# A hybrid layer's state-space part: a second unit's input in lent tiles, a shorter step table, and one GELU in place

## The chip, the cores and the metric

The kernel runs on one core of one Trainium2 chip. Its engines work side by side, each through its own list of instructions: PE (TensorE) multiplies matrices, DVE (VectorE), ACT (ScalarE) and POOL (GpSimd) do elementwise work, and SP (SyncE) issues transfers (DMAs). POOL and ACT may issue transfers too. An engine that waits holds back all that is queued behind on its own list. What counts is the time of one execution on the device, in microseconds (us). Weight loads of PE are listed as PEld.

## The reference

One layer with 2048 frames, 1024 channels and float32 values. Two groups of heads share one normalisation and one input projection; their outputs share an output projection.

```python
h = rmsnorm(x, norm_mix_g[l])
proj = h @ w_in[l]                       # 512 columns u, then q, k, v of 512 each
y_ssm = s5_mixer(u_ssm, ...)
y_att = chunked_attention(q, k, v, attn_rel_bias[l])
mixed = concatenate([rmsnorm(y_ssm, ...), rmsnorm(y_att, ...)])
x = x + mixed @ w_out[l]
h2 = rmsnorm(x, norm_ffn_g[l])
x = x + (silu(h2 @ w_gate[l]) * (h2 @ w_up[l])) @ w_down[l]
return rmsnorm(x, norm_final_g)
```

The state-space mixer is a complex diagonal recurrence over the frames, then `y = gelu(C x + D u)` and `y * sigmoid(y @ w_glu + b_glu)`. The attention looks at the own chunk of 64 frames and the eight before it, with 8 heads of 64.

## The kernel before

**Stages.** After a prologue (input projection `u`, tables of the recurrence) come the attention with the state-space layer woven into it, then the mix phase (GELU, GLU, output projection), then the feed-forward part.

**Steps.** `att_phase` runs 128 steps: 4 blocks of 512 frames, 4 pairs of heads, 2 heads, 4 tiles of queries. A step issues the scores of its tile (PE `sc`, then DVE L866, which adds the bias and takes the minimum for the exponent, then the exponential on ACT, L869) and the transposes of the step two earlier: PE writes them to the bank `pt`, ACT casts a high part `pth` (L884), DVE subtracts a low part `ptl` (L885). Matrices are multiplied in three products of high and low parts. Products with the values (`pj`) and the scaling of a pair of heads (`rb`, DVE L918, stored to `ya_s` by SP, L919) follow when a head or a pair is through.

**Units.** Everything else that belongs under the attention is cut into `Unit`s: generators with a first and a last step. At each step every unit is advanced in proportion. Projections of the next block (`hT`, `qk`, `v` units), eight pairs of state-space units (`ssm_front`, `ssm_back`) and the start of the mix phase are such units. The tables SX and SY give the first steps of the eight fronts and backs.

A front loads the input `U` (128x1024) and the weights `Bst`, multiplies them (PE `pj<-U,Bst`), copies the result into `X` (ACT L584), and POOL runs the recurrence in place on `X` (L598 to L601 steps of a scan, L609 and L610 carries). At its end POOL issues four transfers of the states into `XG` (L632). The back loads `Tm` and `Vm`, multiplies `U` by `Tm` and `XG` by `Vm` into `pj`, ACT copies the sum over `U` (L652), and SP stores that as `y` (L654). Even units from 2 on keep `U` in the space of `rsn`; all others share one buffer `U`, so that unit 1's load must follow unit 0's store.

**Order.** PE's instructions keep the order of the program. Those of DVE, ACT, POOL and SP are ordered by the Tile framework's scheduler, except where the code pins one. Tiles come from pools; the pool `aw` holds the tiles of the projections, `ssm` those of the state-space units. A pool that is released gives its space to the next.

**Mix phase.** It opens at step 119 (OPEN), where `aw` is released, and advances from step 122 (GSTART) as a unit of 26 parts. `fetch` reads `y` for two blocks of 64 chunks into `yr` (L1038), `load` turns it into `ys` by a GELU that reads with a stride (L1050), then splits `ys` into `gh` and `gl`. `glu` multiplies by `w_glu` (split into `wgh` and `wgl`), applies the sigmoid (L1079) to the whole block and multiplies. Newton steps (L98 to L111) make the inverse root of the mean square for a block, `spread` lays it across partitions by transposes of `no`, `rstd2` multiplies with it, `mixed` splits the result for `w_out`. Block 0's `w_out` starts with two held first halves: PE does the four rows of weights that belong to the attention's output, and the second half when the state-space part is there. ACT applies one function table at a time: changing between the exponential and the GELU shows as ACT_TABLE_LOAD.

Of the kernel before, what the change touches and what calls it, by code (L numbers as in the profile page):

```python
# [34 lines left out]
WB = 3  # L35
OPEN, GSTART = 119, 122
R1 = 13
SGB = 2
RA1, RA2 = 2, 12
QS = 4, 5, 6, 7, 0, 1, 2, 3  # L40
# [519 lines left out]

def ssm_front(k, p, psum, S, b, eng):

# [15 lines left out]
    for q in range(GP):  # L578
        ps = k.t(psum, "pj", [P, 2, NC], bufs=2)
        for g2 in range(2):  # L580
            k.ta.matmul(ps[:, g2, :], bst[:, 2 * q + g2, :], U[:, 2 * q + g2, :], start=True, stop=True)
        for g2 in range(2):
            for c in range(2):
                nc.scalar.copy(X[g2 * NS : (g2 + 1) * NS, c, q, :], ps[c * NS : (c + 1) * NS, g2, :])  # L584
        yield
# [74 lines left out]
ST = 2, 10  # L660
SX = 4, 24, 35, 48, 61, 74, 87, 100
SY = 20, 36, 49, 62, 75, 88, 101, 114

# [23 lines left out]
def att_phase(k, ident, S, aw, x0, roots):  # L687

    tc, nc, io, pfs = k.tc, k.nc, k.io, k.pfs
    with ExitStack() as cx:  # L690
# [265 lines left out]
        for b in range(NG // GB):  # L956
            units.append(Unit(ssm_front(k, sp, psum, S, b, k.ssm_eng), SSM_F, SX[b], SX[b] + 9, SX[b] - 2 if b == 0 else 2 if b == 1 else 5, light=SL))
# [23 lines left out]

PY, PZ = 8, 1
MIX_N = 17 + PY + PZ


def mix_phase(k, S, bank):
# [3 lines left out]
    with ExitStack() as cx:  # L990
# [48 lines left out]

        def load(sb, one=False):  # L1040
            b = B()
            b.o = {}
            yt = k.t(my, "ys", [P, 4, SB], bufs=2)
            b.ys, b.g = [yt[:, f] for f in range(4)], []
            if sb and sb % 2 == 0:
                fetch(sb)
            yv = b.yr = yrs[0][:, :, :, (sb % 2) * 64 : (sb % 2 + 1) * 64]
            fs = [slice(0, 4)] if one else [slice(f, f + 1) for f in range(4)]
            for s in fs:
                nc.scalar.activation(yt[:, s].rearrange("p f (c j) -> p f c j", j=L), yv[:, s].rearrange("p f j c -> p f c j"), AF.Gelu_apprx_tanh)  # L1050
            for f in range(4):
# [48 lines left out]
        def big():  # L1100
            return k.t(psum, *BIG)
# [42 lines left out]
        def next_block(sb):  # L1144
            b = load(sb)
            load_a(b, sb)
# [18 lines left out]
        b = load(0, True)  # L1165
        load_a(b, 0)
        raws = [load_wo(n, wr, "xt") for n in range(2)]
        for _ in range(PY):
            yield
        for n, _ in enumerate(glu(b, bank, True)):  # L1170
            if n == RA1:
# [5 lines left out]
            yield  # L1177
        nxt = load(1, True)
        for _ in range(PZ):
            yield  # L1180

# [16 lines left out]
        for sb in range(NSB):  # L1198
# [3 lines left out]
            if sb == 0:  # L1202
                held = [w_out(0, b, 2 * n) for n in range(2)]
                next(held[0])
                ps = big()
                spread(k, te, ps[:, :512], b.o[1], 0)
                with tc.high_priority():
                    rstd2(b, 1, ps[:, :512])
                    mixed(b, 1)
                next(held[1])  # L1210
            else:
                mixed(b, 1)
            for n in range(4):
                if n == 0 and 0 < sb < NSB - 1:
                    nxt = next_block(sb + 1)
                if sb or n > 1:
                    for _ in w_out(sb, b, 2 * n):
# [519 lines left out]
```

## Time and profile before

| | us |
|---|---|
| median of three runs | 2264.51 |
| lowest and highest run | 2261.2, 2265.51 |
| the profiled execution, time | 2267.91 |
| the profiled execution, span | 2266.1 |
| PE busy | 2165.6 (96% of the span) |
| DVE busy | 1542.4 (68%) |
| ACT busy | 1003.3 (44%) |
| POOL busy | 351.2 (15%) |

The rows of a timeline read: start in us, duration, engine, line of the kernel, operation, what it writes <- what it reads, shape, how many (xN), and in brackets the engine's idle time ahead of it with what ended it. A row with x5 stands for five instructions in a row. Times of single rows are from the profiled execution.

### The profile page before, as it was taken

What the parts mean: (1) busy time and instruction counts of PE and PEld (TensorE: products, weight loads), DVE (VectorE), ACT (ScalarE), POOL (GpSimd) and SP (SyncE); (2) the same over time, 40 slices, a digit from 0 to 9 for tenths busy, and PEclk for the clock granted to TensorE, in tenths of its full rate; (3) what the DMA queues carried; (4) which work ended last, traced back from release to release, by engine and by line L of the source; (5) the groups of instructions that cost most, each with busy time, mean ns of one, the idle gap of its engine ahead of it and who ended that gap; (6) DMA issues with size and microseconds to landing.
All of it is one profiled execution on the core that took longest, in us unless ns stands there. A gap on an engine that the chain in (4) does not pass through costs nothing.

```text
span 2266.1 us, 30134 instructions
## 1 busy us (share of the span) xinstructions
PE 2165.6 (96%) x10632; PEld 1825.8 (81%) x10632; DVE 1542.4 (68%) x2695; ACT 1003.3 (44%) x1656; POOL 351.2 (15%) x827
## 2 busy tenths in 40 slices
PE   8988899999997899999999999999999999999997
PEld 6777788898986788778888887888888778888886
DVE  7756666556557756776766668766656477688776
ACT  5445555556557442353333335333333443353322
POOL 2246576656500000000000000000000010000000
PEclk9999999999998899999999999999999999999999
DMA  8878876666552435754556457645433395465652
GB/s 276 254 244 261 268 233 207 192 190 205 187 168 100 138 109 188 251 168 144 180 176 209 162 198 269 199 163 190 140 97 112 102 385 182 167 227 181 216 183 75
DMA packets 194903, 430.41 MB, mean 190 GB/s; under 512 B 19904, under 2 KB 38384, under 8 KB 187648
## 3 DMA queue, kind: packets, MB, share of 16 engines
q1 hardware_dynamic: 187104, 403.58, 53.8%
q0 software_dynamic: 7648, 24.92, 3.6%
q8 instruction: 83, 1.36, 0.2%
q14 instruction: 68, 0.56, 0.1%
HBM read 288.95 MB, written 131.10 MB: 185 GB/s over the span
## 4 chain that ended last, share of the span: by engine, by line
PE 78%; DMA 7%; DVE 6%; ACT 3%; issue 2%; SPq 0%; DVEq 0%; ACTq 0%
PE X L76 20%; PE ps L76 17%; PE Y L76 10%; PE pf L76 10%; PE big L76 6%; PE W L76 5%; PE pj L76 4%; PE pt L79 2%; PE sc L76 2%; DMA acc<-x 2%; DMA lo<-hc 1%; DMA xt<-in_xt 1%; DVE lo L153 1%; DMA hc<-gh 1%; DVE ptl L885 1%
## 5 line engine op out<-in xcount | busy, mean ns | idle before, releaser
L76 PE MATMUL X<-hi,c 128*128 128x512 f32 x1408 | 450.8, 391 | 7.4 <-DVE c L153 5.1
L76 PE MATMUL ps<-hd,hd 128*128 128x512 f32 (+1 forms) x1968 | 429.6, 380 | 3.0 <-DVE hd L153 2.0
L76 PEld LDWEIGHTS ps<-hd,hd 128*128 128x128 f32 x1968 | 357.5, 189 | 73.6 <-DVE hd L153 2.7
L76 PEld LDWEIGHTS X<-hi,c 128*128 128x128 f32 x1408 | 265.1, 188 | 64.1 <-DVE c L153 6.0
L76 PE MATMUL X<-lo,c 128*128 128x512 f32 x704 | 274.6, 390 | 0.0
L153 ACT CAST hd<-hd 128x1536 fp32r<-128x1536 f32 (+1 forms) x106 | 147.5, 1394 | 232.5 <-DMA hd<-hq 170.9
L76 PE MATMUL Y<-hi,c 128*128 128x512 f32 x704 | 226.0, 392 | 3.8 <-DVE c L153 2.3
L153 DVE TENSOR_TENSOR hd<-hd 128x1536 fp32r<-128x1536 f32 (+1 forms) x106 | 174.1, 1644 | 36.2 <-ACT hd L153 35.8
L153 DVE TENSOR_TENSOR c<-S,c 128x512 fp32r<-128x512 f32 x176 | 121.0, 688 | 103.6 <-ACT c L153 103.3
L1516 POOL DMA_DIRECT2D hd<-hq x7 | 5.3, 755 | 1173.2 <-PE X L76 1161.5
L1408 ACT COPY u<-X 128x512 f32<-128x512 f32 x132 | 77.4, 587 | 199.9 <-PE X L76 199.9
L153 ACT CAST c<-S 128x512 fp32r<-128x512 f32 x176 | 109.5, 622 | 122.5 <-PE Y L76 63.8
L76 PE MATMUL big<-m,woh 128*128 128x512 f32 x512 | 162.6, 399 | 0.0
L76 PEld LDWEIGHTS Y<-hi,c 128*128 128x128 f32 x704 | 133.3, 189 | 32.4 <-DVE c L153 2.8
L1550 DVE TENSOR_TENSOR acc<-acc,ps 128x512 f32<-128x512 f32 x196 | 130.2, 682 | 41.6 <-PE ps L76 41.3
L76 PEld LDWEIGHTS X<-lo,c 128*128 128x128 f32 x704 | 132.6, 188 | 27.4
L76 PE MATMUL pf<-hi,w 128*128 128x512 f32 x416 | 149.1, 410 | 0.0
L153 ACT CAST c<-raw 128x512 fp32r<-128x512 f32 x132 | 82.2, 622 | 149.1 <-PE Y L76 69.1
L76 PE MATMUL Y<-lo,c 128*128 128x512 f32 x352 | 137.7, 391 | 0.0
L885 DVE TENSOR_TENSOR ptl<-pt,pth 128x640 fp32r<-128x640 f32 (+3 forms) x152 | 98.3, 647 | 56.1 <-ACT pth L884 54.7
L869 ACT ACTIVATE s<-s,mn 128x640 f32<-128x640 f32 (+4 forms) x128 | 98.0, 765 | 64.1 <-DVE mn L866 58.1
L884 ACT CAST pth<-pt 128x640 fp32r<-128x640 f32 (+3 forms) x152 | 83.8, 551 | 85.6 <-PE pt L79 80.9
(448 smaller groups left out, 4274.1 us busy)
## 6 DMA issues: line engine op xcount, KB each, us to landing
w<-wss SPq DMA_DIRECT2D x36, 1024.0 KB, 6.2
hq<-g SPq DMA_DIRECT2D x140, 256.0 KB, 2.1
hd<-hq SPq DMA_DIRECT2D x35, 768.0 KB, 4.4
hd<-wc SPq DMA_DIRECT2D x35, 768.0 KB, 6.0
raw<-in_w_gate SPq DMA_DIRECT2D x44, 512.0 KB, 3.7
raw<-in_w_up SPq DMA_DIRECT2D x44, 512.0 KB, 4.2
wc<-px SPq DMA_DIRECT2D x66, 256.0 KB, 3.1
wss<-w SPq DMA_DIRECT2D x12, 1024.0 KB, 6.5
```

Of the source, the lines that this page charges most:

```text
L76: return self.tc.keep_in_program_order(self.tc.nc.tensor.matmul(*a, **b))
L79: return self.tc.keep_in_program_order(self.tc.nc.tensor.transpose(*a, **b))
L153: return nc.scalar.copy(hi, raw), nc.vector.tensor_tensor(lo, raw, f32(hi), op=ALU.subtract)
L869: nc.scalar.activation(s[:, :nk], s[:, :nk], AF.Exp, bias=mn[:], scale=-1.0, accum_out=sums[sb, pr][:, hh, qp : qp + 1])
L884: nc.scalar.copy(pth[:, a:b, qp, :], pt[:, a:b, :])
L885: nc.vector.tensor_tensor(ptl[:, a:b, qp, :], pt[:, a:b, :], f32(pth[:, a:b, qp, :]), op=ALU.subtract)
L1408: nc.scalar.copy(u[:], ps[:])
L1516: (nc.gpsimd if aside else nc.sync).dma_start(f32(lo), src.rearrange("g p c -> p g c"))
L1550: V.tensor_tensor(a, a, ps[:], op=ALU.add)
```

## The change

Unit 1 no longer waits for the shared buffer: its front reads `U` in two halves into the projection tiles `hi0x` and `lo0x` (each 128x512), and its back, which needs it once more, loads it a second time into `U`, behind `Tm`. The tables SX and SY place the fronts and backs from unit 1 on up to ten steps earlier.

At step 108 (FETCH) the pool of the state-space units is released and a tile `y0` (128x4x8x128) takes its space; four transfers read the first two blocks of `y` into it. Two steps later one GELU works on it in place, contiguous, and keeps its place in the order of ACT's instructions. At step 119 `take(0)` and `take(1)` copy it into the two `ys` by eight strided copies of 128x512 on POOL. `load` only splits. Blocks 2 and 3 keep their GELU on ACT.

The mix phase is a unit of 19 parts from step 121, without its waiting parts; three parts of block 0's GLU run ahead of the loads of `ya`, the two places where `rstd1` and `rstd2` of the attention part stand move from 2 and 12 to 10 and 14, and three first halves of `w_out` are held instead of two, two of them ahead of the spread.

```diff
-OPEN, GSTART = 119, 122
+FETCH, OPEN, GSTART = 108, 119, 121
 R1 = 13
 SGB = 2
-RA1, RA2 = 2, 12
+RA0, RA1, RA2 = 3, 10, 14
...
-def ssm_front(k, p, psum, S, b, eng):
+def ssm_input(S, b, q=slice(0, GP)):
+    return S["u"].rearrange("j (c g) n t -> (j c) g (n t)", c=CH)[:, GB * b : GB * b + GB][:, 2 * q.start : 2 * q.stop]
+
+
+def ssm_front(k, p, psum, S, b, eng, lent):
...
-    U = S["rsn"][:, : GB * NC].rearrange("p (g c) -> p g c", g=GB) if b and b % 2 == 0 else k.t(p, "U", [P, GB, NC])[:]
-    k.U[b] = U
-    load(U.rearrange("p g t -> p (g t)"), S["u"].rearrange("j (c g) n t -> (j c) (g n t)", c=CH)[:, GB * NC * b : GB * NC * (b + 1)])
+    if b == 1:
+        us = [lent(q).rearrange("p (g c) -> p g c", g=2) for q in range(GP)]
+        for q in range(GP):
+            load(us[q], ssm_input(S, b, slice(q, q + 1)))
+    else:
+        U = S["rsn"][:, : GB * NC].rearrange("p (g c) -> p g c", g=GB) if b and b % 2 == 0 else k.t(p, "U", [P, GB, NC])[:]
+        k.U[b] = U
+        us = [U[:, 2 * q : 2 * q + 2] for q in range(GP)]
+        load(U, ssm_input(S, b))
...
+    if b == 1:
+        k.U[b] = k.t(p, "U", [P, GB, NC])[:]
+        nc.sync.dma_start(k.U[b], ssm_input(S, b))
...
-SX = 4, 24, 35, 48, 61, 74, 87, 100
-SY = 20, 36, 49, 62, 75, 88, 101, 114
+SX = 4, 19, 31, 42, 54, 66, 78, 91
+SY = 20, 32, 43, 55, 67, 79, 92, 104
...
+            if s == FETCH:
+                sp.release()
+                k.my0 = tc.alloc_tile_pool(name="my0", reuse_waits="tile", bufs=1)
+                k.y0 = k.t(k.my0, "y0", [P, 4, L, 128])
+                for f in range(4):
+                    nc.sync.dma_start(k.y0[:, f], S["y"][:, f * P : (f + 1) * P, :128].rearrange("j p t -> p j t"))
+            if s == FETCH + 2:
+                tc.keep_in_program_order(nc.scalar.activation(k.y0[:], k.y0[:], AF.Gelu_apprx_tanh))
...
-            if s == GSTART:
-                sp.release()
...
-PY, PZ = 8, 1
-MIX_N = 17 + PY + PZ
+MIX_N = 19
...
-        def load(sb, one=False):
+        def take(sb):
...
-            for s in fs:
-                nc.scalar.activation(yt[:, s].rearrange("p f (c j) -> p f c j", j=L), yv[:, s].rearrange("p f j c -> p f c j"), AF.Gelu_apprx_tanh)
...
+            for f in range(4):
+                yo = b.ys[f].rearrange("p (c j) -> p c j", j=L)
+                if sb < 2:
+                    nc.gpsimd.tensor_copy(yo, yv[:, f].rearrange("p j c -> p c j"))
+                else:
+                    nc.scalar.activation(yo, b.yr[:, f].rearrange("p j c -> p c j"), AF.Gelu_apprx_tanh)
+            return b
...
-        fetch(0)
         load_wg()
+        yrs[0] = k.t(my, "yr", [P, 4, L, 128])
+        b = load(take(0))
+        nxt = take(1)
         yield
+        yield
+        g = glu(b, bank, True)
+        for _ in range(RA0):
+            next(g)
+            yield
+        k.my0.release()
...
-        nxt = load(1, True)
-        for _ in range(PZ):
-            yield
+        load(nxt)
+        yield
...
-                held = [w_out(0, b, 2 * n) for n in range(2)]
+                held = [w_out(0, b, 2 * n) for n in range(3)]
                 next(held[0])
+                next(held[1])
                 ps = big()
                 spread(k, te, ps[:, :512], b.o[1], 0)
...
-                next(held[1])
+                next(held[2])
```

The rows below are lists of instructions in their order, without times. Line numbers of the two programs differ: the exponential is L869 before and L882 after, the cast `pth` L884 and L897, `k` L791 and L804, `yt` L908 and L921.

ACT around step 110, before: exponentials `s`, the cast of keys `k`, the copy `yt` of a head's output and the cast `pth` follow each other.

```order
L869 ACTIVATE s_7430,sm_7175<-s_7430,mn_7431 128x640
L791 CAST k_1559_7137<-pf_7244 64x512
L869 ACTIVATE s_7472,sm_7175<-s_7472,mn_7473 128x640
L908 COPY yt_7494<-pj_7477 64x512
L884 CAST pth_7497<-pt_7499 128x5x128
```

The same place after: the GELU on `y0` (shown as `y_1624`), with a table load on each side.

```order
L882 ACTIVATE s_7456,sm_7259<-s_7456,mn_7457 128x640
L804 CAST k_1593_7239<-pf_7322 64x512
L981 ACT_TABLE_LOAD
L981 ACTIVATE y_1624_7419<-y_1624_7419 128x4096
L882 ACT_TABLE_LOAD
L882 ACTIVATE s_7499,sm_7259<-s_7499,mn_7500 128x640
L921 COPY yt_7521<-pj_7504 64x512
L897 CAST pth_7524<-pt_7526 128x5x128
```

The exponential, `yt` and `pth` that stood behind the `k` cast now stand behind the GELU and its two loads.

ACT at steps 119 to 123, before: the GELU of block 0 (`ys<-yr`) stands ahead of `yt` and `pth`, and a load of the exponential's table ahead of the next `s`.

```order
L869 ACTIVATE s_7982,sm_7946<-s_7982,mn_7983 128x640
L1050 ACT_TABLE_LOAD
L1050 ACTIVATE ys_8026<-yr_7910 128x2048
L153 CAST wgh_1710_7915<-sg_7917 128x512
L153 CAST wgh_1713_7921<-sg_7923 128x512
L908 COPY yt_8007<-pj_7990 64x512
L884 CAST pth_8010<-pt_8012 128x5x128
L153 CAST gh_1742_8028<-ys_8026 128x512
```

The same stretch after, from block 0's splits on.

```order
L153 CAST gh_1726_7954<-ys_7949 128x512
L153 CAST gh_1728_7958<-ys_7949 128x512
L804 CAST k_1685_7753<-pf_7806 64x512
L897 CAST pth_7871<-pt_7904 128x5x128
L882 ACTIVATE s_7900,sm_7593<-s_7900,mn_7901 128x640
L153 CAST gh_1730_7962<-ys_7949 128x512
L153 CAST gh_1732_7966<-ys_7949 128x512
L153 CAST wgh_1712_7924<-sg_7926 128x512
L153 CAST wgh_1715_7930<-sg_7932 128x512
L897 CAST pth_7871<-pt_7985 128x5x128
```

No GELU and no table load stand there now; the four casts `gh` are spread between exponentials and `pth` casts.

PE at the spread of block 0's state-space part (`ident` and `no`), before: the first held half (`big_8539`) is done, then the spread, then the second held half.

```order
L76 MATMUL big_8539<-m_1836_8478,woh_1843_8493 128x512 x2
L76 MATMUL big_8539<-m_1836_8478,wol_1844_8494 128x512
L79 MATMUL big_8564<-ident_80,no_8423 128x128 x4
L76 MATMUL big_8587<-m_1833_8469,woh_1837_8481 128x512 x2
L76 MATMUL big_8587<-m_1833_8469,wol_1838_8482 128x512
```

After: the second half (`big_8582`) ends ahead of the spread, and the third (`big_8630`) begins behind it.

```order
L76 MATMUL big_8582<-m_1839_8494,woh_1846_8509 128x512 x2
L76 MATMUL big_8582<-m_1839_8494,wol_1847_8510 128x512
L79 MATMUL big_8607<-ident_80,no_8439 128x128 x4
L76 MATMUL big_8630<-m_1836_8485,woh_1840_8497 128x512 x2
L76 MATMUL big_8630<-m_1836_8485,wol_1841_8498 128x512
```

So one more half stands ahead of the spread, and one still behind it.

More of the change, by code (lines that the diff above doesn't have):

```diff
@@ L580, in ssm_front @@
         for g2 in range(2):
-            k.ta.matmul(ps[:, g2, :], bst[:, 2 * q + g2, :], U[:, 2 * q + g2, :], start=True, stop=True)
+            k.ta.matmul(ps[:, g2, :], bst[:, 2 * q + g2, :], us[q][:, g2, :], start=True, stop=True)
         for g2 in range(2):
@@ L956, in att_phase @@
         for b in range(NG // GB):
[L957 removed]
+            units.append(Unit(ssm_front(k, sp, psum, S, b, k.ssm_eng, lambda q: f32(k.t(aw, ("hi0x", "lo0x")[q], [P, SB], F32R)[:])), SSM_F, SX[b], SX[b] + 9, SX[b] - 2 if b == 0 else 4, light=SL))
             units.append(Unit(ssm_back(k, sp, psum, S, b), SSM_B, SY[b], SY[b] + 2, 6, light=SL))
@@ L1044, in load @@
             b.ys, b.g = [yt[:, f] for f in range(4)], []
-            if sb and sb % 2 == 0:
+            if sb < 2:
+                yv = k.y0[:, :, :, sb * 64 : sb * 64 + 64]
+            elif sb == 2:
                 fetch(sb)
-            yv = b.yr = yrs[0][:, :, :, (sb % 2) * 64 : (sb % 2 + 1) * 64]
-            fs = [slice(0, 4)] if one else [slice(f, f + 1) for f in range(4)]
-            for s in fs:
-                nc.scalar.activation(yt[:, s].rearrange("p f (c j) -> p f c j", j=L), yv[:, s].rearrange("p f j c -> p f c j"), AF.Gelu_apprx_tanh)
+            b.yr = yrs[0][:, :, :, (sb % 2) * 64 : (sb % 2 + 1) * 64]
+            for f in range(4):
+                yo = b.ys[f].rearrange("p (c j) -> p c j", j=L)
+                if sb < 2:
+                    nc.gpsimd.tensor_copy(yo, yv[:, f].rearrange("p j c -> p c j"))
+                else:
+                    nc.scalar.activation(yo, b.yr[:, f].rearrange("p j c -> p c j"), AF.Gelu_apprx_tanh)
+            return b
+        def load(b):
             for f in range(4):
@@ L1144, in next_block @@
         def next_block(sb):
-            b = load(sb)
+            b = load(take(sb))
             load_a(b, sb)
```

7 lines of the change are left out of this document (2 added, 5 removed).

## The prediction, made before the result was known

> **What bounds the kernel now.** I read the windows by stage first, to see where TensorE (PE) is not busy, then the waits of PE there, then the timeline around each wait. Windows by stage (start:end and length in us, then busy time of PE, PE's weight loads, DVE, ACT and POOL, the granted clock, DMA share, GB/s):
>
> ```profile
> 420.00:665.00 245.00, 244.68 (x1554) 224.17 (x1553) 134.04 (x243) 135.82 (x269) 134.36 (x342) 1.00 0.60 184
> 665.00:746.00 81.00, 55.89 (x290) 45.79 (x289) 61.65 (x120) 62.25 (x84) 0.00 (x0) 0.88 0.43 140
> 680.00:700.00 20.00, 8.91 (x40) 7.59 (x40) 12.59 (x21) 18.16 (x26) 0.00 (x0) 0.66 0.28 94
> ```
>
> PE is the bound from 420 to 665 (0.3 us idle of 245), so nothing that merely moves there gains. From 665 to 746, where the attention ends and the mix phase begins, 25.1 of 81 us are idle and the clock falls to 0.88. In 680 to 700 it is ACT that is full (18.16 of 20). PE's waits between 660 and 746 (total, times, longest), and where they end on its timeline:
>
> ```profile
> PE pt L79 <- DVE ptl L885: 13.8, 3, 6.4
> PE big L79 <- DVE no L110: 7.9, 1, 7.9
> ...
> 683.69 1.30 PE L79 MATMUL pt<-ident,s 128*128 128x128 f32 x5 [6.41 <-DVE ptl L885]
> 691.81 1.30 PE L79 MATMUL pt<-ident,s 128*128 128x128 f32 x5 [5.76 <-DVE ptl L885]
> 719.29 0.62 PE L79 MATMUL pj<-ident,rb 128*128 128x128 f32 x4
> 745.83 0.45 PE L79 MATMUL big<-ident,no 128*128 128x128 f32 x1 [7.93 <-DVE no L110]
> ```
>
> `ptl` is the low part of transposed probabilities; DVE makes it from ACT's `pth`. So behind these waits I look at ACT, where both GELUs lie:
>
> ```profile
> 675.15 1.28 ACT L1050 ACT_TABLE_LOAD   x1 [0.30 <-DMA yr<-y]
> 676.45 3.69 ACT L1050 ACTIVATE ys<-yr 128x2048 f32<-128x2048 f32 x1
> 686.67 1.28 ACT L869 ACT_TABLE_LOAD   x1
> ...
> 692.62 3.80 ACT L1050 ACTIVATE ys<-yr 128x2048 f32<-128x2048 f32 x1
> ```
>
> ACT stands in program order: the first GELU waits there for the `yr` DMA, and the casts that PE needs stand behind it. The second GELU is framed by table loads like the first, so the two make 3.69 + 3.80 + 4 x 1.28 = 12.6 us of ACT.
>
> **The change, part by part.**
>
> *A. The GELUs leave the transition (gain).* The gaps of 6.41 and 5.76 us are 12.2. The twelve or so splits and casts of `gh`, `wgh` and the squares still stand between the exponentials, and one or two of them (about 0.6 us each, like the `k` cast below) may still hold an exponential back; I leave 1.3 us for that: −10.9. What these casts read, the POOL copies, comes long before (B). The last scale matmul of the head pair (`pj<-ident,rb`, 719.29) then comes near 708.4.
>
> Next the `spread` at 745.83, which waited 7.93 us for `no`, the end of the Newton steps of block 0's state-space output. SP's rows, ACT's and DVE's on the way there, and matmuls ahead of and behind the gap:
>
> ```profile
> 688.38 37.05 SPq L919 DMA_DIRECT2D ya_s<-ya  x2
> 725.48 3.05 SPq L1010 DMA_DIRECT2D m<-in_w_out  x4
> 730.34 1.05 ACT L153 CAST woh<-m 128x1024 fp32r<-128x1024 f32 x1 [2.67 <-DMA m<-in_w_out]
> 734.52 0.15 DVE L102 TENSOR_SCALAR nv<-big 128x4 f32<-128x4 f32 x1
> ...
> 711.25 0.40 PE L76 MATMUL pf<-gl,wgh 128*128 128x512 f32 x1
> 711.48 0.40 PE L76 MATMUL pf<-gh,wgl 128*128 128x512 f32 x1
> ...
> 747.57 0.63 PE L76 MATMUL big<-m,wol 128*128 128x512 f32 x1
> ```
>
> SP holds the loads of `w_out` (`m`) behind the store `ya_s` of the last head pair until 725.4; ACT waits for them; and DVE, in order, has the first Newton step at 734.52 behind the subtractions that follow these casts. So the chain runs from the scale at 719.29 over SP to the spread, 26.5 us, and the change shortens nothing in it: the spread comes 10.9 earlier, the gap stays, but a third held first half of `w_out` now stands ahead of it on PE. That is 24 matmuls (4 rows of weights, 2 columns, 3 products) at a spacing of 0.23.
>
> 24 x 0.23 = −5.5, work that came after the wait and now fills it. The gap left is about 2.4 us, and I expect the slow stretch behind it (some 8 matmuls of 0.63 instead of 0.40) to go: −1.8. Together A = −18.2. Bounds: 0 (the chain waits for something else) and −25.1 (no idle time left).
>
> The Trainium skill, in "TensorE: Matmul & The Clock Gate", Part 1, says that PE runs its first 3.4 us or so after idling at half its clock; the 0.63 us behind the long gap agrees, and the rule also says that the new gap at step 110 (B) might cost as much once more.
>
> *B. One GELU at step 110 (cost).* Here PE has no idle time to lose it in. ACT and PE there, and POOL's end of the scan:
>
> ```profile
> 622.73 0.58 ACT L791 CAST k<-pf 64x512 fp32r<-64x512 f32 x1
> 625.00 0.83 ACT L869 ACTIVATE s<-s,mn 128x640 f32<-128x640 f32 x1 [1.68 <-DVE mn L866]
> ...
> 627.06 0.69 ACT L884 CAST pth<-pt 128x640 fp32r<-128x640 f32 x1
> ...
> 629.54 0.71 PE L79 MATMUL pt<-ident,s 128*128 128x128 f32 x5
> ...
> 717.99 1.92 ACT L1079 ACTIVATE yr<-yr 128x2048 f32<-128x2048 f32 x1
> ...
> 44.55 0.57 ACT L477 COPY pb<-pp 128x512 f32<-128x512 f32 x1
> 45.15 1.19 ACT L478 COPY rsn<-pb 128x512 f32<-128x512 f32 x1
> ```
>
> By the order of the program the GELU stands behind the `k` cast, so ACT reaches it at 623.3. Its size is 128x4096. The contiguous sigmoid does 2048 in 1.92; the strided GELU does 2048 in 3.69, and a strided copy costs twice the plain one (1.19 to 0.57), so it is the stride and not the function that doubles it. In place there is none: 2 x 1.92 less one fixed part = 3.6 us (bounds 3.6 and 2 x 3.69 = 7.4). With two loads, 1.28 + 3.6 + 1.28 = 6.2 us: ACT is free at 629.5 to 630 instead of 625.0. Then exponential, `yt`, `pth` (0.8 + 0.2 + 0.6 + 0.7) and `ptl` (0.8) end near 632.7, and the transposes of 629.54, which need the `pt` bank back, come 3.1 us late; the next ones, with ACT's backlog of a step, 2.0 more; slow clock about 0.9. B = +6. Bounds: +3 (ACT's 1.7 us idle ahead of 625.00 and others soak it up) to +10 (strided price, or `y0` landing late).
>
> "ScalarE: Activation LUTs" of the Trainium skill, on the pipeline, has one element per cycle and lane whatever the function, 0.833 ns: an estimate of 3.4 us for 4096. The sigmoid agrees (0.94 ns), the strided GELU does not (1.80). With the strided price the sum would be −12 in place of −16.
>
> SP's rows of such loads and of the `ya` load:
>
> ```profile
> 665.37 4.77 SPq L1038 DMA_DIRECT2D yr<-y  x4
> 673.58 2.01 SPq L1060 DMA_DIRECT2D ya<-ya_s  x4
> ```
>
> Four issues of 1.2 us and 4.8 us to landing (as XG's, R3) are 9.6 us. Unit 7's back, whose store they must follow, is through in step 105, some four steps of 4.4 us (R3) ahead of the GELU; with 5 us for that store to land, 15 of 17 us are used, so I count no wait for `y0` and leave a late one to the bound. The four loads leave SP at 665, where what is queued behind them (`sg`, `ya`) moves up by up to 4.8 us.
>
> The POOL copies into `ys`, eight of 128x512, have no row; POOL does nothing from 665 to 746 by the window above, and its 128x434 operation took 1.07 us (below): 8.6 us, or twice if strided. The first four stand right behind the GELU, and are over by 640, where the first GELU of before came at 676. The second four must wait for space that opens at 665; block 1 needs them about as much later as the GELU at 692.62 came behind that at 676.45, 16 us. I take 0, bound +5 (below).
>
> *C. The tables SX, SY move the scan earlier (small).* In the first 420 us there are waits that depend on what collides:
>
> ```profile
> 245.65 0.77 PE L76 MATMUL pj<-U,Bst 128*128 128x256 f32 x1 [4.04 <-DMA Bst<-bsts]
> 289.43 1.33 PE L79 MATMUL pt<-ident,s 128*128 128x128 f32 x5 [3.12 <-DVE ptl L885]
> 385.25 0.64 PE L76 MATMUL sc<-k,q2h 128*128 128x320 f32 x1 [4.08 <-DVE k L792]
> ...
> 284.89 2.14 DVE L744 SCALAR_TENSOR_TENSOR raw<-raw,g_mix,rsn 128x512 f32<-128x512 f32 x1
> 381.49 2.99 DVE L746 TENSOR_TENSOR lo<-raw,hi 128x512 fp32r<-128x512 f32 x2
> ...
> 381.09 1.37 POOL L610 TENSOR_TENSOR X<-X,fx 128x434 f32<-128x434 f32 x1
> 622.61 1.07 POOL L610 TENSOR_TENSOR X<-X,fx 128x434 f32<-128x434 f32 x1
> ```
>
> 245.65 is unit 1's front, which waited for its buffers' loads; with U in lent tiles its load can start earlier, `Bst` as before: of 4.04 I take back 2. At 284.89 and 381.49 DVE's work for the next block's `hT` falls onto POOL's long carries (2.14 and 1.5 us for operations that take about 0.8 and 0.7); the new tables part these: −3 and −5 (with the short gap behind). They make the same collision for `hT(3)` with unit 6: +3. The second load of U is one DMA more: +1. Waits for XG (below) in one or two backs: +2. Sum C = −2 −8 +3 +1 +2 = −4; bounds −12 and +5.
>
> **Sum.** −18.2 + 6 − 4 = −16.2 against the profiled execution's 2267.9 gives 2251.7. That execution is 3.4 us above the median of 2264.5, so I write 2248 against the median. A difference under 0.2% (4.5 us) can hardly be told from none here.
>
> **The rivals.**
>
> *R1, half of it:* ACT and DVE stay full at steps 119 to 123 (splits of both blocks, squares, exponentials), and the load of `ya`, which now waits for the eighth POOL copy, comes later than its 673.6. Then only the first gap goes with its clock (−6.4), −5.5 for the held half, +6, −2: about −8, 2256. For it: 18.16 of 20 us of ACT, of which the second GELU and its loads are only some 7. Against: nothing the attention needs stands behind a DMA on ACT any more.
>
> *R2, no change:* the Newton chain is late whatever precedes it: the loads of `w_out` and the 8 subtractions among which it stands are put off by work that the change moves there (the splits of block 1 on ACT and DVE), and the gain of the two gaps is waited off ahead of the spread; the loss of 6 at step 110 stands against −5.5: 2264. Against it: the chain starts at PE's own last scale.
>
> *R3, slower: the scan becomes the bound.* Tile XG and tile X, what their engines waited for:
>
> ```profile
> L76 PE MATMUL pj<-U,Bst x40: 377/379/767, 160.7 to 586.4; 128*128 128x256 f32 x40
> L632 POOL DMA_DIRECT2D XG<-X x32: 598/622/697, 202.8 to 627.3; - x32
> DMA to landing us min/median/max: 2.3/4.8/8.8
>   ACT X L584: 165.2, 8
> ```
>
> The last unit's matmuls end at 586.4 and its last XG is issued at 627.3 and lands 5.4 later: 46 us. Fronts of steps 4 and 100 span 160.7 to 586.4, 4.4 us a step, and after the change 12 to 14 steps lie between front and back: 53 to 62 us. So 7 us at the tightest. POOL waited 165 us for new fronts, seven of them: 23 a unit, of which the steps cut, 1.5 per unit, take 6.6. It decides once a unit's chain is over 53 to 56 us, that is 15 to 20% longer by collisions with DVE (POOL's 1.37 against 1.07 is 28%, on the share that collides). Then PE, in program order, stops at each of seven backs: at 3 to 4 us each +25, which makes 2273. "SBUF — State Buffer" of the Trainium skill (what contends) has DVE and GpSimd lock a port pair for the whole instruction, the other blocked; the longer DVE and POOL rows side by side bear it out, and it speaks for this rival where the new tables lay carries beside two-input DVE work.
>
> **How the numbers follow.** Forecast 0.64 (2238 to 2256), R1 0.16 (2253 to 2260), R2 0.08 (2260 to 2268), R3 0.08 (2268 to 2285), something unseen 0.04, as likely slower. From these: faster 0.82, same 0.08, slower 0.10. The range, 2237 to 2261, leaves out R3, most of R2 and the tails of the rest, near 2 in 10. Its ends are A at −23 with C at −10, and R1 with B at its upper bound.
>
> **What would show it.** Right: in the stretch from 660 to the spread, the waits for `ptl` fall from 13.8 to under 3 us and no ACT_TABLE_LOAD lies in it ahead of the sigmoid; the wait for `no` is 1 to 4 us, with three held halves ahead; near 629 a new PE wait of about 3 us and a GELU row of 3.6 us on 128x4096; ACT loads fall by three; the 4 us waits at 245 and 385 shrink. Wrong: waits of PE for `pj<-XG,Vm` at several backs (R3); `ptl` waits that remain at 670 to 700 with ACT full (R1); a wait for `no` over 10 us (R2); a GELU of 7 us.

## The result

Over 21 runs each the median fell from 2264.51 us to 2258.93: a ratio of 0.9973, with an interval of 0.9962 to 0.9983, so 4 to 9 us, where 16 were forecast. The direction held and the time lies in the stated range, but the size was three times too large.

The profile of the changed kernel shows much more than that, and must be read with care: it is of an execution of 2249.97 us, the lowest of the 21, while that of before, 2267.91, lies above its median. Its rows at the places of the prediction (PE's waits and their ends, then ACT):

```profile
PE pt L79 <- DVE ptl L898: 7.1, 1, 7.1
PE sc L76 <- DVE k L805: 3.3, 1, 3.3
...
PE sc L76 <- DVE mn L879: 4.1, 2, 3.0
PE pj L76 <- DVE ptl L898: 2.2, 1, 2.2
PE pt L79 <- DVE ptl L898: 1.8, 2, 1.3
PE pt L79 <- DVE nf L108: 1.0, 1, 1.0
PE big L79 <- DVE no L110: 0.9, 1, 0.9
```
```profile
637.69 1.30 PE L79 MATMUL pt<-ident,s 128*128 128x128 f32 x5 [7.14 <-DVE ptl L898]
742.65 0.62 PE L79 MATMUL big<-ident,no 128*128 128x128 f32 x4 [0.93 <-DVE no L110]
...
628.35 1.28 ACT L981 ACT_TABLE_LOAD   x1 [4.20 <-DMA y<-y]
629.65 3.62 ACT L981 ACTIVATE y<-y 128x4096 f32<-128x4096 f32 x1
633.28 1.28 ACT L882 ACT_TABLE_LOAD   x1
```

The first fence is the waits of PE, from 415 to 665 above its mark and from 665 to 760 below it. The two long waits for `ptl` at the transition are gone, the wait for `no` fell from 7.9 to 0.9 us, and one of 7.1 us stands at step 111 behind the GELU, which takes 3.62 us as forecast. Not forecast is ACT's wait of 4.20 us for `y0` ahead of the GELU's table load. ACT's table loads fell from 15 to 13 in all, not by three. Windows of the same two stages as before:

```profile
420.00:665.00 245.00, 234.42 (x1482) 214.71 (x1481) 131.46 (x235) 137.10 (x263) 111.48 (x272) 0.99 0.60 180
665.00:746.00 81.00, 70.77 (x366) 60.04 (x365) 66.88 (x129) 53.86 (x86) 4.28 (x4) 0.94 0.41 142
```

PE's idle time in the transition fell from 25.1 to 10.2 us; the stage ahead of it, which had 0.3 us, now has 10.6, nearly all of it the 7.1 behind the GELU and 3.3 for `k`.

To compare executions that differ by more than the change does, I split the time up to PE's last instruction in three: the gaps between PE's instructions (idle); for the records of the granted clock at 0.5, half of the time in them in which PE was not idle (half clock); and the rest.

| us | before | before again | after | after again |
|---|---|---|---|---|
| the profiled execution's span | 2266.1 | 2264.4 | 2248.0 | 2260.7 |
| idle | 93.2 | 89.6 | 83.4 | 84.6 |
| half clock | 26.8 | 30.6 | 19.7 | 29.6 |
| the rest | 2138.8 | 2136.8 | 2137.5 | 2139.1 |

The rest is the same work. Idle time differs by 5 to 10 us between the kernels and by 1 to 4 within one. The half clock differs by 10 us between two executions of the same program, and that is most of what makes the first profile of after look so good.

### The profile page after: what moved, and what is told of

Read it like the earlier page. It is cut to its first block, busy times and chain, and to the rows that moved or that the text cites. A ratio compares the mean times of both kernels' runs of the same rounds, so it can differ in the third digit from the quotient of the medians.

```text
span 2248.0 us, 30147 instructions
## 1 busy us (share of the span) xinstructions
PE 2157.2 (96%) x10632; PEld 1821.4 (81%) x10632; DVE 1540.6 (69%) x2695; ACT 995.8 (44%) x1653; POOL 370.0 (16%) x835
## 4 chain that ended last, share of the span: by engine, by line
PE 77%; POOL 5%; DVE 5%; DMA 4%; issue 3%; ACT 2%; SPq 0%; DVEq 0%; ACTq 0%; POOLq 0%
PE X L76 20%; PE ps L76 18%; PE Y L76 10%; PE pf L76 8%; PE big L76 8%; PE W L76 5%; PE pj L76 3%; PE sc L76 2%; PE pt L79 2%; DMA hd<-wc 1%; POOL X L611 1%; POOL X L610 1%; POOL st L608 1%; POOL st L609 1%; POOL X L620 1%
## 5 line engine op out<-in xcount | busy, mean ns | idle before, releaser
L882 ACT ACTIVATE s<-s,mn 128x640 f32<-128x640 f32 (+4 forms) x128 | 98.0, 766 | 66.4 <-DVE mn L879 61.9
L897 ACT CAST pth<-pt 128x640 fp32r<-128x640 f32 (+3 forms) x152 | 83.7, 551 | 85.9 <-PE pt L79 81.5
## 6 DMA issues: line engine op xcount, KB each, us to landing
hq<-g SPq DMA_DIRECT2D x140, 256.0 KB, 2.1
wc<-px SPq DMA_DIRECT2D x66, 256.0 KB, 3.2
```

The source lines that it names most:

```text
L882: nc.scalar.activation(s[:, :nk], s[:, :nk], AF.Exp, bias=mn[:], scale=-1.0, accum_out=sums[sb, pr][:, hh, qp : qp + 1])
L897: nc.scalar.copy(pth[:, a:b, qp, :], pt[:, a:b, :])
```

## The experiments

Medians stand against 2263 to 2265 us for the kernel before in the same sessions, and ratios go against it.

**The changed kernel again**, for a typical profile; no edit.

> The changed kernel once more, unchanged, for a second profile of it. Theory 1 (the sum was right in its terms, but the profiled execution of after was a lucky one): this profile has a span of 2254 to 2261 us, and the 8 to 10 us more than the 2248.0 lie in stretches the change doesn't touch or in waits for DMA. Theory 2 (the gain is real and steady at 16 to 18 us, and the 21 runs had a drift): median near 2250 and a span near 2248.

Measured: 2257.49 us, ratio 0.9979 (0.9968 to 0.9991); the profile's span is 2260.7. Theory 1 holds in that the first profile was a lucky one and the gain is 5 to 6 us, not 16; that the sum was right in its terms does not follow. The 12.7 us between the two profiles are 9.9 of half clock, 1.2 of idle time and 1.6 of the rest. Windows of this execution around one place:

```profile
744.50:747.90 3.40, 1.39 (x9) 1.25 (x9) 3.16 (x9) 1.97 (x4) 0.00 (x0) 1.00 0.94 258
747.90:751.30 3.40, 3.40 (x9) 2.64 (x8) 3.40 (x6) 3.09 (x6) 0.00 (x0) 0.50 1.03 330
746.00:960.00 214.00, 210.54 (x944) 174.16 (x945) 143.15 (x317) 89.13 (x127) 0.00 (x0) 0.96 0.56 179
```

and of the first profile of after, at the same wait:

```profile
739.20:742.60 3.40, 2.52 (x12) 1.75 (x10) 3.37 (x9) 1.48 (x4) 0.00 (x0) 1.00 0.50 135
742.60:746.00 3.40, 3.35 (x17) 2.86 (x18) 3.19 (x6) 3.01 (x5) 0.00 (x0) 1.00 1.06 341
746.00:960.00 214.00, 209.92 (x974) 173.83 (x973) 147.11 (x324) 91.00 (x131) 0.00 (x0) 1.00 0.57 185
```

The wait for `no` (2.0 us in one, 0.9 in the other) left PE busy for 1.39 of 3.4 us and was followed by 3.4 us at half clock in the one; in the other PE was busy for 2.52 and the clock stayed up. The last row of each fence is the stretch behind the wait: a mean clock of 0.96 in place of 1.00 over 214 us is some 8.6 us, most of the 9.9.

**The GELU left out.**

```diff
-            if s == FETCH + 2:
-                tc.keep_in_program_order(nc.scalar.activation(k.y0[:], ...))
```

> The changed kernel without the GELU of the first two blocks at step 110 (left out, so that the output is not the reference's): the two table loads around it go as well. Theory 1 (the step-110 GELU costs what its profile shows, 8.8 us between steps 108 and 112, in place of the 6 of the prediction): 2250 us, 9 below the changed kernel. The prediction's size: 2253. Rival (the loss there is waited away again later, because the transition is paced by something else): 2257 to 2259.

Measured: 2248.78 us, ratio 0.9934 (0.9922 to 0.9947): 8.7 below the changed kernel of the same session. Theory 1. The windows say the same:

```profile
600.00:640.00 40.00, 40.00 (x271) 37.41 (x270) 23.55 (x44) 22.53 (x45) 4.46 (x4) 1.00 0.68 195
```

PE has no idle time there without the GELU. In the two profiles of the changed kernel (the second, the first) steps 108 to 112, counted from DVE's minimum of the one to that of the other, are 7.9 and 8.7 us longer than here: 5.7 and 7.1 us of it are idle, 2.5 and 1.5 half clock.

**The tables alone**, in the kernel before, with the lent tiles that they need.

```diff
-SX = 4, 24, 35, 48, 61, 74, 87, 100
-SY = 20, 36, 49, 62, 75, 88, 101, 114
+SX = 4, 19, 31, 42, 54, 66, 78, 91
+SY = 20, 32, 43, 55, 67, 79, 92, 104
...
+        us = [lent(q) ... for q in range(GP)]
...
-... SX[b] - 2 if b == 0 else 2 if b == 1 else 5, light=SL))
+... SX[b] - 2 if b == 0 else 4, light=SL))
```

The last two lines are part of the change as well, though its diff above leaves them out: the fronts' loads are issued four steps ahead, where it was two for unit 1 and five for the later ones.

> The kernel before with only the lent tiles for unit 1 and the new tables SX and SY; GELUs, mix phase and held halves as before. Theory 1 (by the marks of the two profiles up to step 108, +0.8 us): 2263 to 2266. The prediction's term C: -4, so 2260. Rival (the tables themselves cost what is missing, about 10 us): 2272 or more.

Measured: 2268.64 us, ratio 1.0015 (1.0002 to 1.0029): 3.4 us slower by the ratio, 5.3 by the medians. The prediction's −4 falls, and the rival's 10 too. That the tables lose anything is barely clear of noise; that they don't gain the forecast 4 is clear. PE's waits from 200 to 540 in this kernel, to be read against those of before in the second fence:

```profile
PE pt L79 <- DVE ptl L898: 6.1, 8, 1.2
PE pf L76 <- DMA w<-wss: 3.5, 2, 2.4
PE sc L76 <- DVE k L805: 3.2, 1, 3.2
PE pj L79 <- ACT X L594: 2.5, 2, 2.4
```
```profile
PE pt L79 <- DVE ptl L885: 6.4, 5, 3.1
PE sc L76 <- DVE k L792: 4.1, 1, 4.1
PE pj L76 <- DMA Bst<-bsts: 4.0, 1, 4.0
PE sc L76 <- issue: 2.2, 1, 2.2
PE pj L76 <- ACT X L584: 0.8, 1, 0.8
```

Each of the three waits that the prediction wrote off is gone (4.0 for `Bst`, 4.1 for `k`, 3.1 for `ptl`), and others stand in their place: `w`, whose load on SP now stands behind unit 2's (`Bst` at 255.2, `w` at 256.0), 3.5; `k` at the new collision, 3.2; `X`, 2.5; more short ones for `ptl`. Idle time up to step 108 is 45.1 us here, 45.0 and 42.7 in the two profiles of before, and 43.4 and 45.7 in the two of after. This profile (2264.65 us) is of a run below its kernel's median, so where the last 3 us lie isn't shown.

**The loads of `y0` earlier.**

```diff
-FETCH, OPEN, GSTART = 108, 119, 121
+FETCH, OPEN, GSTART = 106, 119, 121
...
-            if s == FETCH + 2:
+            if s == 110:
```

> The changed kernel with the loads of y0 written two steps earlier (step 106 in place of 108), the GELU still at step 110. Theory 1 (ACT's 4.2 us wait for y0 ahead of the GELU's table load is there in most executions and PE pays for it): 3 to 5 us faster than the changed kernel, 2254 to 2256, and the wait gone from ACT's timeline. Rival (PE's stall there is set by the GELU's own 6.2 us, and the wait is hidden, or the loads land late wherever they are issued): the same as the changed kernel, 2258 to 2260.

Measured: 2258.41 us, ratio 0.9972 (0.9960 to 0.9985), the same; but ACT's wait for `y0` is still 4.18 us, and SP still issues the second pair of loads at 624.8, 11 us ahead of the GELU's table load, since the scheduler sets its order. The edit did not bring the loads forward, so the run does not test what an earlier `y0` is worth; its wait and PE's stall behind it, 7.12 us, are used further down.

**The GELU two steps later.**

```diff
-            if s == FETCH + 2:
+            if s == FETCH + 4:
```

> The changed kernel with the GELU on y0 two steps later (step 112), its loads where they were. Theory 1 (ACT's wait of 3 to 4 us for the loads of y0, longer in landing than the prediction counted, is what makes the GELU cost 9 us in place of 6): the wait is gone, PE's stall falls from 6 or 7 to about 3 us, 3 to 5 us faster than the changed kernel, 2254 to 2255. Rival (the stall is set by the 6.2 us of the GELU with its tables wherever it stands): the same as the changed kernel, 2257 to 2260, and PE's stall again 6 to 7 us.

Measured: 2259.26 us, ratio 0.9973 (0.9959 to 0.9987). The rows of this kernel on ACT:

```profile
640.80 0.37 ACT L839 CAST v<-pf 128x256 fp32r<-128x256 f32 x1
641.19 1.28 ACT L981 ACT_TABLE_LOAD   x1
642.48 3.62 ACT L981 ACTIVATE y<-y 128x4096 f32<-128x4096 f32 x1
646.12 1.28 ACT L882 ACT_TABLE_LOAD   x1
```

The wait for `y0` is gone, and PE's stall is 5.3 us all the same, with 1.9 at half clock. Theory 1's 3 us did not come, and the time is the rival's. But the GELU stands at another place here: ACT goes from the cast of `v` into the table load without a gap, where at step 110 it had 1.68 us idle ahead of the next exponential (the prediction's row at 625.00). So a block of 6.2 us on ACT can make such a stall without any wait; that the wait costs nothing at step 110 does not follow.

**Units 5 and 6 earlier.**

```diff
-SX = 4, 19, 31, 42, 54, 66, 78, 91
+SX = 4, 19, 31, 42, 54, 65, 76, 91
```

> The changed kernel with two entries of the table SX lower: unit 5's front from step 65 in place of 66 and unit 6's from 76 in place of 78, so that unit 6's carries on POOL end ahead of DVE's subtractions for the next block at step 86. Theory 1 (the stall of 3.2 us near 526, which the changed kernel has and the kernel before has not, is the collision of the two): the stall is gone and no other comes, 3 to 5 us faster, 2253 to 2256. Rival (unit 6's front is now too close behind unit 5's scan, and PE waits there instead, or the stall has another cause): the same or slower, 2258 to 2262.

Measured: 2256.98 us, ratio 0.9967 (0.9956 to 0.9979). The wait for `k` at 526 fell from 3.3 to 1.8 us, so the collision is its cause in part. The waits for `ptl` between 200 and 540 grew to 9.1 us in its place, from 5.3 and 6.4 in the two profiles of after. Idle time up to step 108 stayed at 45.3 us, and the gain over the changed kernel (1 to 2 us) is within the uncertainty.

**Two held halves.**

```diff
-                held = [w_out(0, b, 2 * n) for n in range(3)]
+                held = [w_out(0, b, 2 * n) for n in range(2)]
                 next(held[0])
-                next(held[1])
```

> The changed kernel with two held first halves of w_out in place of three (one ahead of the spread, as before). Theory 1 (the third half fills the wait for the Newton steps, as the prediction had it): the wait for no ahead of the spread is 6 to 7 us instead of 1 to 2, and the kernel 5 to 6 us slower than the changed one, 2263 to 2265. Rival (the chain to the spread starts earlier in the changed kernel, and the half fills nothing): the same, 2257 to 2260.

Measured: 2268.23 us, ratio 1.0019 (1.0009 to 1.0030): 10 us slower than the changed kernel, with this at the spread:

```profile
747.22 1.09 PE L79 MATMUL big<-ident,no 128*128 128x128 f32 x4 [7.29 <-DVE no L110]
```

Theory 1, and more than its 5 to 6 us. Without this half the change would be slower than the kernel before.

**The kernel before again**; no edit.

> The kernel before once more, unchanged, for a second profile of it and to see what the comparison gives for no change. Theory 1 (idle time of PE is the same in each execution of one kernel within 2 us, and what differs from run to run is the number of stretches of 3.4 us at half clock): idle 92 to 95 us in all, the remainder of the span differing by the clock alone; median 2262 to 2266, ratio within 0.1% of 1. Rival (idle times themselves differ by 5 us or more): idle outside 90 to 97.

Measured: 2262.78 us, ratio 1.0001 (0.9987 to 1.0015). Idle 89.6 us is outside the 92 to 95 of theory 1 and just outside the rival's 90; it differs by 3.6 us between the two executions, the half clock by 3.8. So both differ from run to run.

**Unit 1's front alone**, with the lent tiles and the lead of four steps, in the kernel before.

```diff
-SX = 4, 24, 35, 48, 61, 74, 87, 100
+SX = 4, 19, 35, 48, 61, 74, 87, 100
...
+        us = [lent(q) ... for q in range(GP)]
```

> The kernel before with the lent tiles and only unit 1's front moved (step 24 to 19); all other entries of SX and SY as before. Theory 1 (the waits that the tables bring near 260, 326, 400 and 526 come from the moves of units 2 to 7, and the lent tiles themselves gain the 4 us wait at 245): 2259 to 2261, 3 to 5 us faster than before, and no wait for Bst at 245. Rival (the second load of U or the earlier front costs what the wait gave): 2263 to 2266. The prediction's term for this part alone: -2 + 1 = -1, so 2262 to 2263.

Measured: 2265.22 us, ratio 1.0002 (0.9992 to 1.0012). The wait for `Bst` is gone; 1.1 for `w`, 1.8 for `mn` and more for `ptl` took its place. The rival holds: no gain of lending by itself can be seen, though the prediction's −1 us for this part is too small to be ruled out.

**The GELUs out of the transition**, in the kernel before (POOL copies in their place, the GELU of two blocks left out).

```diff
-                nc.scalar.activation(yt[:, s]..., yv[:, s]..., AF.Gelu_apprx_tanh)
+                if one:
+                    for f in range(4):
+                        nc.gpsimd.tensor_copy(b.ys[f]..., yv[:, f]...)
```

> The kernel before with the GELU of the first two blocks left out (the output is not the reference's): eight copies on POOL, at the GELUs' places in the mix phase, take their place; two GELUs of 3.7 us and their table loads leave ACT's transition. Theory 1 (the two stalls of 6.4 and 5.8 us are those GELUs'): both stalls under 1.5 us, 11 to 14 us faster than before, 2250 to 2253. Rival (ACT is full there anyhow, or the spread's wait grows by what is gained): 2257 to 2262.

Measured: 2256.53 us, ratio 0.9965 (0.9953 to 0.9976): 8.1 us by the medians, short of theory 1. Its PE waits:

```profile
PE big L79 <- DVE no L110: 7.6, 1, 7.6
PE pt L79 <- DVE ptl L885: 4.1, 2, 3.3
PE sc L76 <- DVE mn L866: 2.1, 3, 1.1
PE pf L76 <- DVE sq L1027: 1.5, 1, 1.5
```

Of 13.8 us of waits for `ptl`, 4.1 stay, and 1.5 for the squares come new; the wait for `no` did not grow. But most of the 4.1 belongs to this kernel alone: ACT's casts `gh` wait 3.6 us in all for the copies that POOL makes at that very place, and PE's stall stands behind them.

```profile
675.64 0.62 ACT L153 CAST gh<-ys 128x512 fp32r<-128x512 f32 x1 [1.92 <-POOL ys L1052]
680.05 0.77 PE L79 MATMUL pt<-ident,s 128*128 128x128 f32 x5 [3.26 <-DVE ptl L885]
```

In the changed kernel the copies come earlier (633.3 and 665.8), and no such wait is there.

**A third held half**, in the kernel before.

```diff
-                held = [w_out(0, b, 2 * n) for n in range(2)]
+                held = [w_out(0, b, 2 * n) for n in range(3)]
                 next(held[0])
+                next(held[1])
```

> The kernel before with a third held first half of w_out, ahead of the spread, and nothing else. Theory 1 (the wait of 7.9 us for no takes 5.5 us of it, and the half clock behind the wait goes in part): 5 to 8 us faster, 2256 to 2259, the wait 2 to 3 us. Rival (the half's weights come too late or the spread is put off by PE): 2262 to 2266.

Measured: 2256.95 us, ratio 0.9968 (0.9957 to 0.9980), 7.7 us faster, with the wait at 2.6:

```profile
745.81 0.68 PE L79 MATMUL big<-ident,no 128*128 128x128 f32 x4 [2.62 <-DVE no L110]
```

Theory 1. This one part, without the lent tiles, the tables and the moved GELU, gives the time of the whole change within the uncertainty.

**Loads two steps ahead**, with units 5 and 6 moved as above.

```diff
-... SX[b] - 2 if b == 0 else 4, light=SL))
+... SX[b] - 2 if b == 0 else 4 if b == 1 else 2, light=SL))
```

> The changed kernel with units 5 and 6 moved as in the run with two lower entries of SX, and the loads of units 2 to 7 issued two steps ahead of their front in place of four. Theory 1 (the two waits of 1 and 2.3 us for w near 260 come from loads of unit 2 that stand ahead of w on SP): they are gone, 3 to 5 us faster than the run with the two entries alone, 2252 to 2254. Rival (the fronts now wait for their own loads): 2258 or more, with waits for Bst or U.

Measured: 2255.08 us, ratio 0.9960 (0.9944 to 0.9976). The waits for `w` are gone, and 3.8 us for `X` and 0.9 for `Bst` came; 2 us less than without the edit, within the uncertainty.

**Unread matmuls in the stall**, in the changed kernel.

```diff
                 elif o == "t" and LAG <= s < N + LAG:
+                    if s == 111:
+                        wm = k.t(psum, "pj", [P, 512], bufs=2)
+                        for _ in range(24):
+                            k.ta.matmul(wm[:], hT[3][0][7][:, :P], hT[3][0][7], start=True, stop=True)
```

> The changed kernel with 24 more matmuls of 128x512, which nobody reads, ahead of the transposes that PE waits for at step 111, behind the GELU. Theory 1 (about 2 to 3 us of the GELU's cost are PE at half clock behind its stall of 6 us): the matmuls take 5.5 us of the stall, no stretch of half clock stands behind it, 2 to 4 us faster than the changed kernel, 2254 to 2256. Rival (the clock behind the stall costs nothing, since ACT's backlog holds PE anyhow): the same, 2257 to 2260; if the matmuls come on top of the stall, 2262.

Measured: 2255.9 us, ratio 0.9964 (0.9950 to 0.9977), 2 to 3 below the changed kernel. The stall's place in its timeline:

```profile
632.84 5.64 PE L76 MATMUL pj<-hi 128*128 128x512 f32 x24
639.51 0.74 PE L79 MATMUL pt<-ident,s 128*128 128x128 f32 x5 [1.02 <-DVE ptl L898]
```

The matmuls fill the stall, and no half clock is recorded behind it: the transposes take 0.74 us where they took 1.30. Steps 108 to 112 are 21.1 us in place of 22.3 and 23.1, in line with theory 1, though the medians alone would not show it beyond their uncertainty.

**Half of the GELU later**, in the changed kernel.

```diff
-tc.keep_in_program_order(nc.scalar.activation(k.y0[:], k.y0[:], ...))
+tc.keep_in_program_order(nc.scalar.activation(k.y0[:, :, :, :64], ...))
...
+            if n == 13:
+                tc.keep_in_program_order(nc.scalar.activation(nxt.yt[:], nxt.yt[:], AF.Gelu_apprx_tanh))
```

> The changed kernel with the GELU at step 110 only on block 0's half of y0 (in runs of 64), and block 1's half done in place in ys, behind the last exponential and ahead of the sigmoid of block 0. Theory 1 (PE's stall at step 110 goes with the length of ACT's block, and ACT has 3 to 5 us to spare behind the last exponential): the stall is 1.8 us shorter, the GELU of block 1 with its table load costs at most 1 us, so 1 to 2.5 us faster than the changed kernel, 2256 to 2257.5. Rival (the second GELU puts off the splits of block 1 and the sigmoid, and the chain to the spread with them): 2260 to 2263.

Measured: 2258.93 us, ratio 0.9972 (0.9961 to 0.9982). The stall at step 111 is 4.3 us, behind a wait of 3.1 for `y0`: less that wait it is 1.1 where it was 2.9, so it follows the length of ACT's block; between the last exponential and the spread PE now waits 1.5 us for `pth`, 1.2 for `ya` and 2.3 for `no`, 1 us more than before the edit, and the median is that of the changed kernel.

**The same in the kernel with units 5 and 6 moved and shorter lead**; the edits of both.

> The same split of the GELU in the kernel with units 5 and 6 moved and the loads of units 2 to 7 two steps ahead. Theory 1: 1 to 2.5 us faster than that kernel (2255.1), 2252.5 to 2254. Rival, as above: 2256 to 2259.

Measured: 2257.06 us, ratio 0.9970 (0.9959 to 0.9982): no gain over that kernel.

**All of these together**; the edits of the last three.

> That kernel with the 24 unread matmuls at step 111 as well. Theory 1: 3 to 6 us faster than the kernel with the moved units alone (2255.1), 2249 to 2252, if the stall that is left is still near 5 us; the matmuls, longer than a shorter stall, would take the gain of the halves back, 2252 to 2254. Rival: 2256 or more.

Measured: 2255.57 us, ratio 0.9956 (0.9944 to 0.9969). The ratio is the lowest of all kernels that compute the reference, some 0.2% below the changed kernel's, and its interval overlaps that one's. The three edits don't add up to what was expected of them.

## Why the prediction was off

| term | forecast | measured | by |
|---|---|---|---|
| A, the GELUs leave the transition | −10.9 | −8.1 | GELUs out of the kernel before |
| A, the third held half and the clock behind it | −7.3 | −7.7 | third half in the kernel before |
| B, the GELU at step 110 | +6 | +8.7 | GELU left out of the changed kernel |
| C, lent tiles and tables | −4 | +3.4 | tables alone (ratio) |
| sum | −16.2 | −3.7 | whole change: −5.6 by the medians |

The parts sum to −3.7 against −5.6. With an uncertainty of about 3 us each they agree with the whole, and can't show more than that; the third half, for one, is worth 7.7 us in the kernel before and 10 in the changed one.

- **A, mechanism right, size a little high.** The step "I leave 1.3 us for that" failed. In the changed kernel PE's idle time between step 112 and the spread, the wait for `no` left out, fell from 17.2 to 9.3 us: 7.9 in place of 10.9. I had counted one or two casts on ACT; the largest wait that came, 3.0 us, stands behind the splits on DVE:

```profile
676.96 1.28 DVE L153 TENSOR_TENSOR wgl<-sg,wgh 128x512 fp32r<-128x512 f32 x2
678.76 0.81 DVE L879 CUSTOM_DVE_ANT_0 s<-sc,nba 128x640 f32<-128x640 f32 x1
679.64 0.64 PE L76 MATMUL sc<-k,q2h 128*128 128x320 f32 x1 [2.98 <-DVE mn L879]
```

The third half was priced right within the uncertainty, and the chain behind the spread nearly so: from the last scale to the spread it is 24.4 and 25.1 us after and 26.2 before. The 1.8 for the clock behind the spread came in the first profile and not in the second, so this part is chance.
- **B, the wait for `y0` left out.** The GELU's 3.6 us, its tables and its place were right. The failed step is "so I count no wait for `y0`". In the six profiles with the whole GELU at step 110 and nothing put into the stall, PE's stall is ACT's wait for `y0` and 2.9 us more:

| us | ACT's wait | PE's stall | difference |
|---|---|---|---|
| after | 4.20 | 7.14 | 2.94 |
| after again | 2.78 | 5.72 | 2.94 |
| loads of `y0` earlier | 4.18 | 7.12 | 2.94 |
| units 5 and 6 earlier | 3.57 | 6.51 | 2.94 |
| two held halves | 3.69 | 6.64 | 2.95 |
| loads two steps ahead | 3.51 | 6.45 | 2.94 |

So the step by which the transposes "come 3.1 us late" was well priced: without the wait, an estimate from this table is 2.9 us. No run had `y0` there in time at step 110, so it stays an estimate. The wait comes on top, us for us. Rows of the second profile:

```profile
630.55 1.28 ACT L981 ACT_TABLE_LOAD   x1 [2.78 <-DMA nba<-nbs]
639.89 1.30 PE L79 MATMUL pt<-ident,s 128*128 128x128 f32 x5 [5.72 <-DVE ptl L898]
```

The profile puts this wait down to `nba`, but `nba` landed at 630.90, when the table load was running; the last load of `y0` landed at 630.30. I had 9.6 us from the first issue of these loads to the last landing. In the first profile it is 17 us, from 611.3 to 628.1:

```profile
611.34 1.46 SPq L979 DMA_DIRECT2D y<-y  x2
...
618.02 1.24 SPq L979 DMA_DIRECT2D y<-y  x2
```

SP issued loads of `k`, `q2h` and `q2l` and a store between the two pairs, and the last load took 9.6 us to land. The "2.0 more" for the next transposes did not come, and the half clock was 1.5 to 2.5 us in place of 0.9. With A's GELU term, moving the GELU is a trade of 8 for 9 us.
- **C, no gain.** This is the largest miss. The waits were seen rightly and went away; the step that failed is that I wrote them off as a gain and counted one new collision (3, measured 3.2). The loads and carries that are shifted meet other work of the same density: `w` behind unit 2's loads (3.5), `X` (2.5). Idle time up to step 108 stayed the same.
- **The base.** The sum went against one profile, and the half clock alone differs by 4 us between the two executions of before and by 10 between those of after, more than the whole effect. That the changed kernel's first profile fell at 2250, near the sum's 2248 to 2252, was chance.
- **The rivals.** R1's time (2256) is the nearest. Of its mechanism the late `ya` did not come (ACT waited 0.6 us for it), and the full DVE came in small, as the 3.0 us above. R2's wait for `no` shrank. R3 did not come: no back waited for XG in the changed kernel, and the scan still ended ahead.

## What to carry to other kernels

Moving a block of work from a place where PE already waits to one where PE is full trades a stall for a stall. Price it by the engine's whole block less the slack that this engine and those behind it have at the new place: 6.2 us of ACT made a stall of 2.9 at step 110 by the estimate above, and of 5.3 two steps later. Then add in full the time by which the block's input lands late, and to find that, ask what else stands between its loads in the issuing engine's order. A wait in a crowded stage that a shift removes is a gain only if the shifted loads and operations have somewhere empty to go. What held its price within the uncertainty was independent PE work, already there, set ahead of a wait; try that first, alone.

## What the runs showed of the hardware

In these traces PE's granted clock is 1 or 0.5, in stretches of 3.41 us or multiples of it, on a grid that is steady within an execution and starts at another point in each one (only the last stretch, at the program's end, is of another length). Over all eighteen profiles, the stretches of each grid that ran at full clock can be counted by how long PE was busy in them. Of 149 with PE busy for under 0.4 of the stretch, all were followed by one at half clock; of 64 between 0.4 and 0.5, 43 were; of 108 between 0.5 and 0.6, 13; of 236 between 0.6 and 0.8, 3. A stretch at half clock that is full of work costs 1.7 us, half of its 3.41. So a wait of 2 us costs 2 or nearly 4 us by where it falls on the grid (1.39 of 3.4 us busy and 2.52 of 3.4 above), and one execution's profile says little about effects below 10 us. "TensorE: Matmul & The Clock Gate" of the Trainium skill (Part 1, on what is actually happening) has this free-running window of 3413 ns, and says that how many matmuls run slow differs from run to run with its phase; the traces agree.

A few such stretches (33) stand where the records show PE busy for over 0.8 of the stretch ahead, nearly all at the same three places of the program (near 760, 820 and 880 us), as in the changed kernel's second profile:

```profile
765.00:768.40 3.40, 2.80 (x21) 2.57 (x20) 2.67 (x7) 0.63 (x1) 0.00 (x0) 1.00 0.32 119
768.40:771.80 3.40, 3.40 (x10) 2.62 (x9) 3.40 (x28) 1.69 (x2) 0.00 (x0) 0.50 0.78 189
```

What brings these on was not settled.
